# A two-layer hybrid trunk: fewer buffers for split expert weights, more for loaded ones, and attention values with V as the stationary operand

## The chip, the core and the metric

The kernel runs on one core of a Trainium2 chip as one program. The metric is device microseconds of that core, from the start of an execution to its end. Five engines work beside each other: TensorE (PE, with its weight loads shown apart as PEld), VectorE (DVE), ScalarE (ACT), GpSimd (POOL) and SyncE (SP, which issues most DMA transfers).

## The reference, cut to what matters

256 latent and 256 context tokens of width 1024 pass through two layers. Each layer mixes tokens with three groups of heads, and then applies a SwiGLU: a dense one in layer 0, the two best of eight experts in layer 1. The part of the mixer that the change touches, and the expert part:

```python
def gqa_attention(q, k, v):            # 8 query heads, 2 key/value heads, head width 64
    scale = GQA_HEAD_DIM ** -0.5
    def block(qb):
        s = jnp.einsum('bqgrd,bkgd->bgrqk', qb, k) * scale
        p = jax.nn.softmax(s.astype(jnp.float32), axis=-1).astype(v.dtype)
        return jnp.einsum('bgrqk,bkgd->bqgrd', p, v)
    return sweep_query_blocks(block, q)

def moe_swiglu(t, router, wg, wu, wd):
    ...
    for e in range(N_EXPERTS):
        out = out + gates[:, e:e + 1] * swiglu(t, wg[e], wu[e], wd[e])
```

Latent queries read all 512 keys, context queries only the 256 context keys. Layer 1 has latent queries only.

## The kernel before, in words

**Accuracy.** Operands of the large products are split into a high and a low part of type fp32r, and a product is three matmuls (`mm3`, L242 to L245). Softmax weights and values are plain fp32; a plain fp32 matmul is two records (two weight loads and two matmuls) in the trace.

**Grouped-query attention (GQA).** A unit is one query tile (128 queries), one head: 16 units with 512 keys and 16 with 256 in layer 0, 16 with 512 in layer 1. A unit goes through stages of a software pipeline (`staged`, lags 0, 2, 4, 5): `g_scores` computes scores with two matmuls, the first over 128 rows (q high and low against k high, L697), the second over 64 rows (q high against k low, L698), then DVE takes the maximum (L441), ACT the exponential with its sum (L442); `g_turn` transposes the weights, 128 keys at a time, with PE (L458) and copies them to SBUF, by ACT (L434) and DVE (L436) in turn; `g_values` multiplies (L528): the transposed weights are the stationary operand, the 64 columns of V move, one matmul for each 128 keys. The result has queries on partitions. After eight heads `g_finish` divides by the softmax sums (L716, L718), transposes the result four times (L722), and splits it into `yh` and `yl` (L725, L726), which the output projection reads. `take_gkv` prepares K: it splits it and transposes it (L620 to L634); the low part is kept on 64 partitions only (`kgl`, L576).

The Tile scheduler sets the order of this work on each engine from the order in which the program emits it, with Hyena convolution, the norm of the differential heads and, in layer 0, adaLN products (L261) merged in.

**Experts.** 84 rounds and 5 tail rounds run over 672 loads of 512 KB, all issued by SP into a ring of `RAW` buffers (L49, `raw`). A load comes free for the next when its readers are done. Two loads of a round are split, by ACT (`whi`, L1141) and DVE (`wlo`, L1142), into tiles of a ring of three, for experts with a full tile of 128 tokens; the rest of the work (`mm_few`, L1256 to L1263) reads the raw weights, as the moving operand, against 64 or 32 tokens that are stationary in column parts of the array. In `drive` (L1174 to L1216) the order of PE is written out by hand: in a round PE does the split products of the round before (L243 to L245), then the raw products of this round (L1262), while ACT and DVE split for the next. The first load waits for the router's result (SP L1118 reads `ctli`).

Of the kernel before, what the change touches and what calls it, by code (L numbers as in the profile page):

```python
# [10 lines left out]
F32 = mybir.dt.float32  # L11
F32R = mybir.dt.float32r
I32 = mybir.dt.int32
AF = mybir.ActivationFunctionType
# [14 lines left out]
GH, GKV, GD = 8, 2, 64  # L29
# [16 lines left out]
WIDE = {"B": 128, "A": 64, "C": 32}  # L46


RAW = 14  # L49

UPS = [(0, 1024), (1024, 1024), (2048, 1024), (3072, 512)]

# [2 lines left out]
def trunk(ctx: ExitStack, tc: tile.TileContext, I, out, dbg=None):  # L55
# [25 lines left out]
    def merge(*streams):  # L81

        done = [0] * len(streams)
        while True:
            left = [(done[j] / n, j) for j, (_, n) in enumerate(streams) if done[j] < n]
            if not left:
                break
            j = min(left)[1]
            next(streams[j][0], None)
            done[j] += 1  # L90
        for g, _ in streams:
            run(g)
# [5 lines left out]
    def fr(ap):  # L98
        return ap.bitcast(F32)
# [331 lines left out]
    def evac(dst, src):  # L431
        evac_n[0] += 1
        if evac_n[0] % 2:
            S.activation(dst, src, AF.Copy)  # L434
        else:
            V.tensor_copy(dst, src)  # L436
# [28 lines left out]
    def etile():  # L465
        blocks[0] += 1
        if blocks[0] % 9 < 5:
            return wk.tile([128, 512], F32, name="e", tag="e", bufs=5)
        return half_of("aTl").rearrange("p c q -> p (c q)")
# [9 lines left out]
    def keys_of(s):  # L479
        return (0, 4) if s == 0 else (2, 2)  # L480

    def mixer(i, u, streams, pools, begun, first, extra):
# [75 lines left out]
        def d_values(s, qt, h):  # L558
# [4 lines left out]
            if h == DH - 1:  # L563
# [9 lines left out]

        keys = (ap_l if streams == 2 else hp).tile([128, 2, GKV, 512], F32R, name="keys",
                                                   tag="keys" if streams == 2 else "H1")
        kg, kgl = keys[:, 0], keys[0:64, 1]  # L576
        gv = ap_l.tile([128, 4, GKV * GD], F32, name="gv", tag="gv")
        gt_ = [None, None]
        qg = []
# [39 lines left out]

        def take_gkv(t, ps):  # L620
            r = head_norm(ps[:, 0:128].rearrange("p (h d) -> p h d", d=GD), GKV, t, 1)
            st = wk.tile([128, 6, GD], F32R, name="kst", tag="kst", bufs=2)
            s2 = st[:, 0:4].rearrange("p (h a) d -> p h a d", a=2)
            S.activation(s2, r[:, :, None, :].to_broadcast([128, GKV, 2, GD]), AF.Copy)
            V.tensor_sub(st[:, 4:6], r, fr(s2[:, :, 0]))
            ps2 = bank("t", F32R)
            for m in range(2):
                PE.transpose(ps2[:, 128 * m:128 * m + 128], st[:, 2 * m:2 * m + 2].rearrange("p a d -> p (a d)"),
                             identr)
                PE.transpose(ps2[0:64, 256 + 128 * m:384 + 128 * m], st[:, 4 + m], identr)  # L630
            tk = slice(128 * t, 128 * t + 128)
            evac(kg[:, :, tk], fr(ps2[:, 0:256]).rearrange("p (m q) -> p m q", q=128))
            evac(kgl[:, :, tk], fr(ps2[0:64, 256:512]).rearrange("p (m q) -> p m q", q=128))
            evac(gv[:, t], ps[:, 128:256])  # L634

        run(xblock(u, w, OFF_GK, 256, [(t, 0, 256) for t in range(4)], take_gkv))
# [16 lines left out]
        def hy_blocks():  # L653
            for grp in (2, 1, 0):
                pst = [bank("a") for _ in range(2)]
                for k0 in (0, 4):
                    hi, lo = wload(rows_k(w, 256 * grp, 256, k0, k0 + 4), 4, 256)
                    for j in range(2):
                        cs = slice(128 * j, 128 * j + 128)
                        for k in range(4):  # L660
                            mm3(pst[j][:, 0:ntok], (hi[:, k, cs], lo[:, k, cs]),
                                (u[0][:, k0 + k, 0:ntok], u[1][:, k0 + k, 0:ntok]), k0 + k == 0, k0 + k == KC - 1)
                    if k0 == 0:
                        yield
                for j in range(2):
                    ps = pst[j][:, 0:ntok]
                    if grp == 2:
                        short_conv(4 + j, ps, vv[:, j])
                    elif grp == 1:
                        x1 = wk.tile([128, 512], F32, name="x1", tag="t2k", bufs=4)  # L670
                        short_conv(2 + j, ps, x1[:, 0:ntok])
                        V.tensor_mul(vv[:, j], vv[:, j], x1[:, 0:ntok])
                    else:
                        short_conv(j, ps, x0[:, j])
                yield

        ada_tag[0] = "a"
        merge((d_attn, len(d_units) + 3), (hy_blocks(), 6), *extra[0:1])
        qg.append(ap_.tile([128, GH, ntok], F32R, name="qg", tag="X1"))
        for g in range(2):  # L680
            run(xblock(u, w, OFF_GQ + 256 * g, 256, [(t, 0, 256) for t in range(nq)], take_gq(g)))
# [8 lines left out]
        def g_scores(s, qt, h):  # L690
            kt0, nk = keys_of(s)
            n, q0, g = 128 * nk, 256 * s + 128 * qt, h // 4
            keys = slice(128 * kt0, 128 * kt0 + n)
            if h == 0:
                SM[s, qt] = wk.tile([128, GH], F32, name="sm1", tag="sm", bufs=2)
            ps = bank("s")
            PE.matmul(ps[:, 0:n], qg[0][:, h, q0:q0 + 128], kg[:, g, keys], start=True, stop=False)  # L697
            PE.matmul(ps[:, 0:n], qg[0][0:64, h, q0:q0 + 128], kgl[:, g, keys], start=False, stop=True)  # L698
            e = etile()
            softmax_block(ps, n, e, SM[s, qt][:, h:h + 1])  # L700
            E[s, qt, h] = e

        def g_turn(s, qt, h):
            AT[s, qt, h] = to_keys(E.pop((s, qt, h)), keys_of(s)[1])

        def g_values(s, qt, h):
            if h == 0:
                PV[s, qt] = bank("a")
            g = h // 4
            values(PV[s, qt], h, AT.pop((s, qt, h)), gv[:, :, GD * g:GD * g + GD], *keys_of(s))  # L710

        def g_finish(s, qt, h):
            if h < GH - 1:
                return
            sm, ps = SM[s, qt], PV.pop((s, qt))
            V.reciprocal(sm, sm)  # L716
            o = wk.tile([128, 512], F32, name="go", tag="t2k", bufs=4)
            V.tensor_mul(o.rearrange("p (h d) -> p h d", d=GD), ps.rearrange("p (h d) -> p h d", d=GD),  # L718
                         sm[:, :, None].to_broadcast([128, GH, GD]))
            ps = bank("a")  # L720
            for c in range(4):
                PE.transpose(ps[:, 128 * c:128 * c + 128], o[:, 128 * c:128 * c + 128], ident)  # L722
            p3 = ps.rearrange("p (c q) -> p c q", q=128)
            q0 = 256 * s + 128 * qt
            S.activation(yh[:, 4:8, q0:q0 + 128], p3, AF.Copy)  # L725
            V.tensor_sub(yl[:, 4:8, q0:q0 + 128], p3, fr(yh[:, 4:8, q0:q0 + 128]))  # L726
# [409 lines left out]
    newest = [None]  # L1136

    def split_w(raw, a, b):
        hi = mp.tile([128, a, b], F32R, name="whi", tag="whi", bufs=3)
        lo = mp.tile([128, a, b], F32R, name="wlo", tag="wlo", bufs=3)  # L1140
        S.activation(hi, raw, AF.Copy)  # L1141
        newest[0] = V.tensor_sub(lo, raw, fr(hi))  # L1142
        return hi, lo
# [492 lines left out]
```

## Time and profile before

| | us |
|---|---|
| three runs | 1896.03, 1898.89, 1900.34 (median 1898.89) |
| the profiled execution | 1900.39 |
| its span in the trace | 1898.6 |
| PE busy | 1816.5 (96%) |
| DVE busy | 896.3 (47%) |
| ACT busy | 618.9 (33%) |
| GQA of layer 0, with what is merged into it | about 199.8 to 289 |
| GQA of layer 1, with what is merged into it | about 847.4 to 898 |
| loads of the expert part | about 948 to 1871 |

A timeline row gives the start, the length, the engine, the line, the operation, what it writes from what, shapes and a count; what stands in brackets is idle time of that engine ahead of it and what ended it. A row of weight loads (PEld) marks where PE's sequencer has got to, and the distance from one row's start to the next is the pitch. PEclk is the granted clock as a share of full speed.

### The profile page before, as it was taken

How to read it: one execution, taken by the hardware profiler on the slowest of the kernel's cores; microseconds unless marked ns; L12 is line 12 of the kernel's file. 1: busy time of each engine (PE TensorE's matmuls, PEld its weight loads, DVE VectorE, ACT ScalarE, POOL GpSimd, SP SyncE). 2: the span in 40 equal slices, each digit the busy share in tenths (PEclk: the TensorE clock that was granted, in tenths of full speed). 3: DMA queues.
4: the chain of work that ended last, by engine and by line, in shares of the span. 5: the costliest groups of instructions: out<-in, count | busy, mean ns of one | idle time of the engine just before them, and what ended most of it. 6: DMA issues, size and time to landing. Idle time of an engine off the chain costs nothing.

```text
span 1898.6 us, 34294 instructions
## 1 busy us (share of the span) xinstructions
PE 1816.5 (96%) x13638; PEld 1245.6 (66%) x13638; DVE 896.3 (47%) x1507; ACT 618.9 (33%) x1037; POOL 65.0 (3%) x75
## 2 busy tenths in 40 slices
PE   6999999899999998989799999999899999999996
PEld 3778668778888887877666666667555544454442
DVE  3767654765754456686633332323333333233333
ACT  3554433433213334554432222222222222222221
POOL 0200100000000000010000000000000000000002
PEclk9999999999999999999799999999998999999998
DMA  8233323444555553230499999999997999999995
GB/s 317 87 109 112 95 88 130 129 161 144 183 171 167 161 168 111 88 107 18 145 408 407 354 402 373 385 343 364 408 399 268 351 404 404 382 400 409 400 404 200
DMA packets 193631, 481.93 MB, mean 254 GB/s; under 512 B 16911, under 2 KB 59824, under 8 KB 193335
## 3 DMA queue, kind: packets, MB, share of 16 engines
q1 hardware_dynamic: 187929, 471.68, 67.3%
q10 hardware_dynamic: 5246, 6.94, 1.1%
q8 instruction: 109, 1.79, 0.4%
q0 software_dynamic: 288, 1.05, 0.2%
q14 instruction: 59, 0.48, 0.1%
HBM read 474.36 MB, written 5.24 MB: 253 GB/s over the span
## 4 chain that ended last, share of the span: by engine, by line
PE 88%; DVE 4%; DMA 3%; ACT 1%; issue 1%; POOL 1%; SPq 0%; POOLq 0%; DVEq 0%; ACTq 0%
PE ma L1262 24%; PE psa L243 8%; PE psa L245 8%; PE psa L244 8%; PE mb L1262 6%; PE mb L243 4%; PE mb L245 4%; PE mb L244 4%; PE psa L528 3%; PE mq L1440 2%; DMA raw<-in_moe_wd_dram 2%; PE pst L458 2%; PE psa L261 1%; PE mq L1330 1%; PE pss L244 1%
## 5 line engine op out<-in xcount | busy, mean ns | idle before, releaser
L1142 DVE TENSOR_TENSOR wlo<-raw,whi 128x1024 fp32r<-128x1024 f32 x168 | 204.7, 1223 | 300.5 <-ACT whi L1141 283.3
L1262 PE MATMUL ma<-raw,xF 128*32 128x256 f32 (+3 forms) x4352 | 326.2, 385 | 3.7 <-issue 2.9
L1141 ACT ACTIVATE whi<-raw 128x1024 fp32r<-128x1024 f32 x168 | 177.0, 1057 | 379.2 <-PE mb L245 288.3
L1262 PEld LDWEIGHTS ma<-raw,xF 128*32 128x32 f32 (+1 forms) x4352 | 167.2, 115 | 153.5 <-issue 64.1
L235 ACT ACTIVATE whi<-raw 128x1024 fp32r<-128x1024 f32 x120 | 125.3, 1045 | 276.4 <-PE pst L245 84.5
L236 DVE TENSOR_TENSOR wlo<-raw,whi 128x1024 fp32r<-128x1024 f32 x120 | 144.8, 1208 | 118.7 <-ACT whi L235 116.9
L243 PE MATMUL psa<-uh,whi 128*128 128x512 f32 (+1 forms) x448 | 173.1, 388 | 1.8 <-DVE uh L386 1.8
L245 PE MATMUL psa<-uh,wlo 128*128 128x512 f32 (+1 forms) x448 | 171.7, 384 | 2.5 <-DVE wlo L236 2.4
L244 PE MATMUL psa<-ul,whi 128*128 128x512 f32 (+1 forms) x448 | 172.1, 384 | 0.0
L1262 PE MATMUL ma<-raw,hF 128*32 128x256 f32 (+1 forms) x1904 | 165.7, 418 | 6.3 <-DMA raw<-in_moe_wd_dram 5.7
L1262 PEld LDWEIGHTS ma<-raw,hF 128*32 128x32 f32 (+1 forms) x1904 | 73.5, 115 | 89.9 <-issue 32.6
L313 DVE SCALAR_TENSOR_TENSOR acc<-raw,cst,acc 128x512 f32<-128x512 f32 x140 | 98.4, 748 | 28.6 <-DMA raw<-in_w_ada_dram 27.9
L245 PEld LDWEIGHTS psa<-uh,wlo 128*128 128x128 f32 x448 | 84.9, 190 | 20.7 <-DVE wlo L236 5.1
L243 PEld LDWEIGHTS psa<-uh,whi 128*128 128x128 f32 x448 | 85.4, 191 | 19.9 <-DVE uh L386 2.0
L244 PEld LDWEIGHTS psa<-ul,whi 128*128 128x128 f32 x448 | 85.5, 191 | 15.9 <-issue 0.2
L243 PE MATMUL mb<-whi,xB 128*128 128x512 f32 x224 | 95.6, 427 | 0.0
L243 PE MATMUL psa<-whi,uh 128*128 128x256 f32 (+1 forms) x288 | 89.9, 313 | 5.7 <-DVE t L424 3.2
L245 PE MATMUL mb<-whi,xB 128*128 128x512 f32 x224 | 90.5, 404 | 0.0
L244 PE MATMUL mb<-wlo,xB 128*128 128x512 f32 x224 | 90.4, 403 | 0.0
L244 PE MATMUL psa<-wlo,uh 128*128 128x256 f32 (+1 forms) x288 | 88.6, 308 | 1.7 <-DVE wlo L236 1.7
L245 PE MATMUL psa<-whi,ul 128*128 128x256 f32 (+1 forms) x288 | 87.9, 307 | 0.0
L1262 PE MATMUL mb<-raw,xF 128*32 128x256 f32 (+3 forms) x768 | 84.6, 423 | 0.0
(383 smaller groups left out, 2735.9 us busy)
## 6 DMA issues: line engine op xcount, KB each, us to landing
raw<-in_moe_wg_dram SPq DMA_DIRECT2D x224, 512.0 KB, 7.6
raw<-in_moe_wu_dram SPq DMA_DIRECT2D x224, 512.0 KB, 7.6
raw<-in_moe_wd_dram SPq DMA_DIRECT2D x224, 512.0 KB, 9.0
raw<-in_w_ada_dram SPq DMA_DIRECT2D x112, 256.0 KB, 3.8
raw<-in_w_ada_dram SPq DMA_DIRECT2D x40, 512.0 KB, 6.2
raw<-in_w_in_dram SPq DMA_DIRECT2D x36, 512.0 KB, 3.6
raw<-in_ffn_wg_dram SPq DMA_DIRECT2D x22, 512.0 KB, 3.9
raw<-in_ffn_wu_dram SPq DMA_DIRECT2D x22, 512.0 KB, 3.7
```

Of the source, the lines that this page charges most:

```text
L235: S.activation(hi, raw, AF.Copy)
L236: V.tensor_sub(lo, raw, fr(hi))
L243: PE.matmul(ps, l[0], r[0], start=first, stop=False)
L244: PE.matmul(ps, l[0], r[1], start=False, stop=False)
L245: PE.matmul(ps, l[1], r[0], start=False, stop=last)
L313: V.scalar_tensor_tensor(a[:, sl], raw, c, a[:, sl], op0=OP.mult, op1=OP.add)
L458: PE.transpose(ps[:, 128 * c:128 * c + 128], a[:, 128 * c:128 * c + 128], ident)
L528: PE.matmul(ps[:, 64 * h:64 * h + 64], at[:, c], v[:, kt0 + c], start=(c == 0), stop=(c == nk - 1))
L1141: S.activation(hi, raw, AF.Copy)
L1142: newest[0] = V.tensor_sub(lo, raw, fr(hi))
L1262: PE.matmul(o[s * h:s * h + s, n * j:n * j + n], x, w[:, n * h:n * h + n], start=first and j == 0, stop=last, tile_position=(0, s * h), sk ...
L1440: PE.matmul(o, l, m, start=(j == 0), stop=(j == len(ops) - 1))
```

## The change

`RAW` goes from 14 to 16, and the rings of `whi` and `wlo` from three tiles to two. In GQA: the low part of K is kept twice, on all 128 partitions, so the second score matmul has 128 rows; the four transposes of K are of one shape, with one copy instead of two. The weights of four heads (one K/V head) are collected, even heads in one tile and odd heads in another, and only then multiplied: V is now stationary, 64 columns in the left half of the array for even heads and in the right half for odd ones, and 256 columns of weights (two heads of 128 queries) move. The result has head dimensions on partitions, so it isn't transposed; the reciprocals of the sums are instead broadcast by POOL, turned by four fp32 matmuls against the identity, copied, and multiplied in. The diff's core:

```diff
-RAW = 14
+RAW = 16
...
-        kg, kgl = keys[:, 0], keys[0:64, 1]
+        kg, kgl = keys[:, 0], keys[:, 1]
...
-            PE.matmul(ps[:, 0:n], qg[0][0:64, h, q0:q0 + 128], kgl[:, g, keys], start=False, stop=True)
-            e = etile()
+            PE.matmul(ps[:, 0:n], qg[0][:, h, q0:q0 + 128], kgl[:, g, keys], start=False, stop=True)
+            e = wk.tile([128, 512], F32, name="e", tag="e", bufs=5)
...
+            evac(AT[s, qt, h // 4][h % 2][:, 0:nk, h % 4 // 2], ps[:, 0:128 * nk].rearrange("p (c q) -> p c q", q=128))
...
+            for c in range(nk):
+                for p in range(2):
+                    PE.matmul(PV[s, qt][64 * p:64 * p + 64, 256 * g:256 * g + 256], gv[:, kt0 + c, GD * g:GD * g + GD],
+                              at[p][:, c], start=(c == 0), stop=(c == nk - 1), tile_position=(0, 64 * p),
+                              skip_group_check=True)
...
-            o = wk.tile([128, 512], F32, name="go", tag="t2k", bufs=4)
-            V.tensor_mul(o.rearrange("p (h d) -> p h d", d=GD), ps.rearrange("p (h d) -> p h d", d=GD),
-                         sm[:, :, None].to_broadcast([128, GH, GD]))
-            ps = bank("a")
+            rb = wk.tile([128, GH, GD], F32, name="rb", tag="t2k", bufs=4)
+            G.tensor_copy(rb, sm[:, :, None].to_broadcast([128, GH, GD]))
+            pr = bank("a")
             for c in range(4):
-                PE.transpose(ps[:, 128 * c:128 * c + 128], o[:, 128 * c:128 * c + 128], ident)
-            p3 = ps.rearrange("p (c q) -> p c q", q=128)
+                PE.matmul(pr[:, 128 * c:128 * c + 128], rb[:, 2 * c:2 * c + 2].rearrange("p a d -> p (a d)"), ident,
+                          start=True, stop=True)
+            rt = wk.tile([128, 512], F32, name="rt", tag="t2k", bufs=4)
+            evac(rt, pr)
+            V.tensor_mul(rt, rt, ps)
+            p3 = rt.rearrange("p (c q) -> p c q", q=128)
...
-        hi = mp.tile([128, a, b], F32R, name="whi", tag="whi", bufs=3)
-        lo = mp.tile([128, a, b], F32R, name="wlo", tag="wlo", bufs=3)
+        hi = mp.tile([128, a, b], F32R, name="whi", tag="whi", bufs=2)
+        lo = mp.tile([128, a, b], F32R, name="wlo", tag="wlo", bufs=2)
```

**PE in the middle of layer 1's GQA**, before (L697 and L698 are the scores, L458 transposes, L528 values with V moving, L243 and L244 belong to the Hyena convolution, L742 too):

```order
L458 MATMUL pst<-ident,e 128x128 x4
L697 MATMUL pss<-keys,qg 128x512
L698 MATMUL pss<-keys,qg 128x512
L528 MATMUL psa<-gv,two 128x64 x4
L243 MATMUL psa<-vt_7578,c_90 128x256
L243 MATMUL psa<-vt_7578,c_91 128x256
L528 MATMUL psa<-gv,two 128x64
L244 MATMUL psa<-vt_7579,c_90 128x256
L458 MATMUL pst<-ident,two 128x128 x4
```

and after (L709 transposes, L723 values with V stationary, L736 the turned reciprocals; eight L723 belong to four heads):

```order
L723 MATMUL psa<-two,gv 64x256 x3
L709 MATMUL pst<-ident,e 128x128 x4
L697 MATMUL pss<-keys,qg 128x512
L698 MATMUL pss<-keys,qg 128x512
L723 MATMUL psa<-two,gv 64x256 x5
L709 MATMUL pst<-ident,e 128x128 x4
L697 MATMUL pss<-keys,qg 128x512
L698 MATMUL pss<-keys,qg 128x512
L736 MATMUL psa<-ident,rb 128x128 x4
L709 MATMUL pst<-ident,e 128x128 x4
```

Before, values stand in every unit; after, a unit is transposes and scores alone, and values come in pieces once in four units, cut in two here (3 and 5). Over the program there are 160 matmuls L528 of GQA before, and 80 matmuls L723 in 18 pieces after (11 in layer 0, 7 in layer 1).

**PE at the end of layer 1's GQA**, before (L243 to L245 with `whi,yh` open the output projection):

```order
L245 MATMUL psa<-c_91,Y 128x256
L528 MATMUL psa<-gv,two 128x64 x4
L722 MATMUL psa<-ident,go 128x128 x4
L243 MATMUL psa<-whi,yh 128x512
L244 MATMUL psa<-wlo,yh 128x512
```

and after:

```order
L245 MATMUL psa<-c_91,Y 128x256
L723 MATMUL psa<-two,gv 64x256 x8
L736 MATMUL psa<-ident,rb 128x128 x4
L243 MATMUL psa<-whi,yh 128x512
L244 MATMUL psa<-wlo,yh 128x512
```

The last values are twice as many matmuls, and the four matmuls behind them read the sums and not the values.

**ACT in the expert part**, before (L1141 splits, L1398 and L434 copy results of a finished expert block):

```order
L1141 ACTIVATE whi<-raw 128x1024 x2
L1398 ACTIVATE yC<-mb 128x256
L1141 ACTIVATE whi<-raw 128x1024 x2
L1398 ACTIVATE yB<-mb 128x512 x2
L1141 ACTIVATE whi<-raw 128x1024
L434 ACTIVATE ptC<-mq 128x256
```

and after (L1159 splits, L1416 copies):

```order
L1159 ACTIVATE whi<-raw 128x1024 x2
L1416 ACTIVATE yC<-mb 128x256
L1159 ACTIVATE whi<-raw 128x1024
L1416 ACTIVATE yB<-mb 128x512
L1159 ACTIVATE whi<-raw 128x1024
L1416 ACTIVATE yB<-mb 128x512
L434 ACTIVATE ptC<-mq 128x256
```

One split moves behind one copy. On PE and SP the expert part stands in the same order in both.

## Rows read from the trace of the kernel before

**Rows 1.** The page: busy time by engine, and the chain of work that ended last

```profile
PE 1816.5 (96%) x13638; PEld 1245.6 (66%) x13638; DVE 896.3 (47%) x1507; ACT 618.9 (33%) x1037; POOL 65.0 (3%) x75
...
PE 88%; DVE 4%; DMA 3%; ACT 1%; issue 1%; POOL 1%; SPq 0%; POOLq 0%; DVEq 0%; ACTq 0%
```

**Rows 2.** Windows of both layers' GQA; columns as in the first line

```profile
core 0: us, PE busy (x) PEld busy (x) DVE busy (x) ACT busy (x) POOL busy (x), PEclk, DMA share, GB/s
199.80:289.00 89.20, 88.07 (x510) 59.33 (x510) 52.78 (x114) 41.35 (x107) 6.01 (x6) 0.96 0.32 95
847.40:898.00 50.60, 45.43 (x300) 36.37 (x298) 35.84 (x80) 23.97 (x58) 4.04 (x4) 0.93 0.08 25
```

**Rows 3.** PEld timeline in layer 1's GQA: a unit and the start of the next

```profile
871.27 0.97 PEld L528 LDWEIGHTS psa<-gv,two 128*128 128x128 f32 x8 [0.25 <-issue]
872.10 0.48 PEld L458 LDWEIGHTS pst<-ident,two 128*128 128x128 f32 x4
872.54 0.19 PEld L697 LDWEIGHTS pss<-keys,qg 128*128 128x128 f32 x1
872.98 0.18 PEld L698 LDWEIGHTS pss<-keys,qg 64*128 64x128 f32 x1 [0.25 <-issue]
873.41 0.97 PEld L528 LDWEIGHTS psa<-gv,two 128*128 128x128 f32 x8 [0.25 <-ACT Y L769]
```

**Rows 4.** PEld timeline in layer 0's GQA, scores of a unit with 256 keys

```profile
258.40 0.19 PEld L697 LDWEIGHTS pss<-keys,qg 128*128 128x128 f32 x1
258.72 0.18 PEld L698 LDWEIGHTS pss<-keys,qg 64*128 64x128 f32 x1
259.03 0.21 PEld L458 LDWEIGHTS pst<-ident,two 128*128 128x128 f32 x2
```

**Rows 5.** PEld timeline: 128-row fp32r matmuls in sequence, of 256 columns and of 512

```profile
195.03 0.19 PEld L244 LDWEIGHTS psa<-wlo,uh 128*128 128x128 f32 x1
195.15 0.19 PEld L245 LDWEIGHTS psa<-whi,ul 128*128 128x128 f32 x1
...
905.09 0.19 PEld L245 LDWEIGHTS psa<-whi,yl 128*128 128x128 f32 x1
905.32 0.19 PEld L243 LDWEIGHTS psa<-whi,yh 128*128 128x128 f32 x1
```

**Rows 6.** PEld timeline, expert part: fp32 in column halves, 512 columns, then 256

```profile
1565.19 0.14 PEld L1262 LDWEIGHTS ma<-raw,hF 128*64 128x64 f32 x2 [0.29 <-issue]
1565.62 0.14 PEld L1262 LDWEIGHTS ma<-raw,hF 128*64 128x64 f32 x2 [0.29 <-issue]
1566.57 0.19 PEld L243 LDWEIGHTS mb<-whi,xB 128*128 128x128 f32 x1 [0.81 <-issue]
...
1684.85 4.25 PEld L1262 LDWEIGHTS ma<-raw,xF 128*64 128x64 f32 x40
```

**Rows 7.** Timeline at the end of layer 1's GQA, the finish

```profile
896.77 0.68 DVE L718 TENSOR_TENSOR go<-psa,sm 128x512 f32<-128x512 f32 x1
...
897.51 0.42 PEld L722 LDWEIGHTS psa<-ident,go 128*128 128x128 f32 x4 [0.93 <-DVE go L718]
```

**Rows 8.** Groups by shape: POOL's nearest operation of 128x512 in fp32

```profile
L1478 POOL TENSOR_TENSOR fo<-fo,gf 128x512 f32<-128x512 f32 x2 | 2.5, 1268 | 4.0 <-ACT fsq L1477 4.0
```

**Rows 9.** Windows in the expert part (columns as in rows 2)

```profile
1280.00:1290.00 10.00, 10.00 (x142) 6.49 (x146) 3.21 (x4) 2.83 (x5) 0.00 (x0) 1.00 0.80 280
1340.00:1350.00 10.00, 8.11 (x92) 4.00 (x84) 2.79 (x3) 2.48 (x3) 0.00 (x0) 1.00 1.02 407
...
1500.00:1870.00 370.00, 369.85 (x1797) 176.22 (x1794) 118.42 (x133) 92.47 (x118) 1.20 (x3) 1.00 1.02 401
```

**Rows 10.** Timeline in the expert part: a split's two operations

```profile
1568.26 1.06 ACT L1141 ACTIVATE whi<-raw 128x1024 fp32r<-128x1024 f32 x1 [7.54 <-DMA raw<-in_moe_wu_dram]
...
1569.36 2.58 DVE L1142 TENSOR_TENSOR wlo<-raw,whi 128x1024 fp32r<-128x1024 f32 x2 [7.38 <-ACT whi L1141]
```

**Rows 11.** Windows in layer 1's GQA: where the granted clock is low

```profile
850.00:854.00 4.00, 1.50 (x6) 0.95 (x6) 3.41 (x10) 2.48 (x7) 0.90 (x2) 0.73 0.00 0
854.00:858.00 4.00, 4.00 (x15) 2.69 (x16) 2.21 (x5) 1.38 (x3) 1.27 (x2) 0.50 0.00 0
```

More of the change, by code (lines that the diff above doesn't have):

```diff
@@ L621, in take_gkv @@
             r = head_norm(ps[:, 0:128].rearrange("p (h d) -> p h d", d=GD), GKV, t, 1)
[L622 to L625, printed above, removed]
+            st = wk.tile([128, 2, GKV, 2, GD], F32R, name="kst", tag="kst", bufs=2)
+            rr_ = r[:, :, None, :].to_broadcast([128, GKV, 2, GD])
+            S.activation(st[:, 0], rr_, AF.Copy)
+            V.tensor_sub(st[:, 1], rr_, fr(st[:, 0]))
+            sf = st.rearrange("p b h a d -> p (b h) (a d)")
             ps2 = bank("t", F32R)
[L627 to L630, printed above, removed]
+            for m in range(4):
+                PE.transpose(ps2[:, 128 * m:128 * m + 128], sf[:, m], identr)
             tk = slice(128 * t, 128 * t + 128)
-            evac(kg[:, :, tk], fr(ps2[:, 0:256]).rearrange("p (m q) -> p m q", q=128))
-            evac(kgl[:, :, tk], fr(ps2[0:64, 256:512]).rearrange("p (m q) -> p m q", q=128))
+            evac(keys[:, :, :, tk], fr(ps2).rearrange("p (b m q) -> p b m q", m=2, q=128))
             evac(gv[:, t], ps[:, 128:256])
@@ L678, in mixer @@
         merge((d_attn, len(d_units) + 3), (hy_blocks(), 6), *extra[0:1])
+        pair.clear()
+        blocks[0] = 0
         qg.append(ap_.tile([128, GH, ntok], F32R, name="qg", tag="X1"))
@@ L703, in g_turn @@
         def g_turn(s, qt, h):
-            AT[s, qt, h] = to_keys(E.pop((s, qt, h)), keys_of(s)[1])
+            e, nk = E.pop((s, qt, h)), keys_of(s)[1]
+            if h % 4 == 0:
+                AT[s, qt, h // 4] = [wk.tile([128, 4, 2, 128], F32, name="two", tag=tag, bufs=2) for tag in ("aTh", "aTl")]
+            ps = bank("t")
+            for c in range(nk):
+                PE.transpose(ps[:, 128 * c:128 * c + 128], e[:, 128 * c:128 * c + 128], ident)
+            evac(AT[s, qt, h // 4][h % 2][:, 0:nk, h % 4 // 2], ps[:, 0:128 * nk].rearrange("p (c q) -> p c q", q=128))
         def g_values(s, qt, h):
-            if h == 0:
+            if h % 4 < 3:
+                return
+            if h == 3:
                 PV[s, qt] = bank("a")
-            g = h // 4
-            values(PV[s, qt], h, AT.pop((s, qt, h)), gv[:, :, GD * g:GD * g + GD], *keys_of(s))
+            g, at = h // 4, AT.pop((s, qt, h // 4))
+            kt0, nk = keys_of(s)
+            for c in range(nk):
+                for p in range(2):
+                    PE.matmul(PV[s, qt][64 * p:64 * p + 64, 256 * g:256 * g + 256], gv[:, kt0 + c, GD * g:GD * g + GD],
+                              at[p][:, c], start=(c == 0), stop=(c == nk - 1), tile_position=(0, 64 * p),
+                              skip_group_check=True)
         def g_finish(s, qt, h):
```

## The prediction

> **What bounds the kernel now.** I read the page first: PE is busy for 96% of the span, and the chain of work that ended last runs through PE for 88% of it [rows 1]. So a microsecond taken from PE counts unless PE then waits for something else. That is a statement on the whole span, and the change touches three stages, so the windows come next [rows 2]. In layer 0's GQA PE is busy for 88.07 of 89.2 us and DVE for 52.78: there is room under PE. In layer 1's GQA it is 45.43 of 50.6 for PE and 35.84 for DVE: if PE loses 10 us there, the two are equal, and waits between them begin to set the pace. DMA is at 0.32 and 0.08, and bounds neither. The expert part is another matter: PE and the DMA engines are both close to full in most of it, and each has a stretch in which it alone is late [rows 9]: at 1280 to 1290 PE is full and DMA at 0.80, at 1340 to 1350 PE does 8.11 of 10 us and DMA is full. The first expert load waits for the router's result, which lies behind both layers' GQA, so time won in GQA moves the whole expert part forward as it is.
>
> **Scores.** The second score matmul of a unit uses 64 rows of the array. In a unit of layer 1 the weight loads start at 872.54 (L697), 872.98 (L698) and 873.41 (the next): the pair takes 0.87 us, and PE's sequencer stood 0.25 us ahead of L698 and again behind it with no work that it waited for [rows 3]. Where 128-row fp32r matmuls of 512 columns follow each other the pitch is 0.23 [rows 5], so a pair would take 0.46. For 256 keys the pair takes 0.63 (258.40 to 259.03 [rows 4]) against twice 0.12 [rows 5]. After the change both have 128 rows. I take these pitches for the new pair: 32 units save 0.41 us, 13.1, and 16 units save 0.39, 6.2: 19.3 us of PE, 12.8 in layer 0 and 6.6 in layer 1. Bounds: if half of the gap comes from the fp32 neighbours, which stay, 9.7; above, 19.3. I take the upper, since the gap ahead of L698 stands between two matmuls of the same type which differ in rows alone.
>
> The Trainium skill, "TensorEngine Tiling (Array Packing)", Key Properties, says that a change of the tiling mode drains TensorE; the gap ahead of the 64-row matmul agrees with it, and by the rule the upper value is the right one. The same rule speaks against the new values, below.
>
> **Values.** Before, 160 matmuls (L528) are 320 records, eight in a full unit, at a pitch of (872.10 - 871.27) / 8 = 0.104 us [rows 3]: 33.2 us. After, 80 matmuls of 256 columns are 160 records. Before has the same form, fp32 in column halves of the array with 256 columns moving, in the expert part: 40 records in 4.25 us, 0.106 each [rows 6], so 17.0 us. That form is slower by itself at one place: where it ends and a full-array matmul follows, the distance is 0.95 us (1565.62 to 1566.57) instead of the 0.43 from pair to pair (1565.19 to 1565.62) [rows 6], 0.52 lost. The order after has 18 pieces of values, so 18 x 0.52 = 9.4 us. Six of the blocks are cut in two at an odd number, where a matmul has no partner in the other half: its two records then take about 0.42 us instead of 0.21, twelve ends, 2.5 us in all. Sum 28.9, a saving of 4.4 us: 2.8 in layer 0, 1.6 in layer 1. Bounds: with no overlap of the halves every record takes twice as long, 0.21, and the saving turns into a loss of 33.6 + 9.4 - 33.2 = 9.8 us; with free ends of pieces it is 16 us. I stay with 4.4, because the expert part shows this form with these neighbours.
>
> **Finish.** Six times, four transposes become four fp32 matmuls, eight records of 128 columns. Nearest rows: 0.104 for a record of 64 columns [rows 3], so 0.8 us or a little more, against 0.4 for the four transposes: 0.5 x 6 = 3 us more for PE, a third of it in layer 1. DVE has one multiplication as before, and the copy of the turned reciprocals lands on ACT or DVE in turn, 0.6 to 0.7 us. POOL's broadcast has no row; its nearest, 128x512 in fp32, takes 1.27 us [rows 8]. It needs only the sums, which are there when the last exponential is, two or more units ahead of the last values, so it is covered in the middle. At the end of layer 1, where nothing else is left, before shows the multiplication at 896.77 and the transposes at 897.51 [rows 7]; after, the chain behind the last values is multiplication, ACT, DVE, without a turn through PE, but the eight values of 64 columns come later in one piece and at their heels four matmuls. The output projection begins with the first query tile, whose split is long done. I put +1 us there (bounds 0 and +2).
>
> **K's preparation.** Four times a layer: four transposes of one shape, one copy of 512 columns instead of two of 256. Nothing on PE, a few tenths on DVE either way: 0.
>
> **Buffers in the expert part.** Two more raw buffers let two more loads of 512 KB run ahead while PE is the late one (1280 to 1290), and so feed PE two loads longer where DMA is (1340 to 1350) [rows 9]. At 401 GB/s [rows 9] a load takes 1.31 us: at most 2.6 us are won, at least none, if later raw buffers come free later by as much. I take 2. Two split tiles instead of three: a round splits two loads, so the split for a round must now wait until the split products of the round before have read theirs. The split takes 1.06 us on ACT and 2.58 / 2 = 1.29 on DVE [rows 10], for two loads about 3.6 us from the first start to the last end. What covers it is the round's raw products, which PE does in between: in the round around 1560 they end at 1566.57 after about 7 us. So nothing, as long as ACT and DVE are free within some 3 us; without that cover each late microsecond would be paid in 84 rounds. One split also moves behind one ACT copy in the order shown, 0.7 us, covered in the same way.
>
> **The sum.** On PE: 19.3 + 4.4 - 3 = 20.7 us in GQA, 13.6 in layer 0 and 7.2 in layer 1. What is late next: the exponential of a unit needs its maximum from DVE, and PE needs the exponential two units on and a free score bank. A unit of layer 1 shrinks from 2.14 us (871.27 to 873.41 [rows 3]) to about 1.5, and DVE, which had 35.84 us of work in the stage, has that still. So I let a tenth of a microsecond for each of 48 units go back into waits, 5 us, two thirds of it in layer 1. 20.7 - 5 = 15.7; + 2 for the raw buffers, - 1 for the tail of layer 1: 16.7. The profiled execution took 1900.39 (span 1898.6 and 1.8 around it): 1883.7; the median of the runs is 1.5 lower than this execution: 1882.2, say 1882.
>
> **The rivals.**
> *All of PE's gain arrives.* If DVE and ACT never hold PE and pieces of values cost less at their ends: 20.7 + 2.6, and half of the 9.4 at the ends, is 28: 1871. For it: DVE has 36 us of room in layer 0. Against: layer 1.
> *PE waits for DVE and ACT, or its clock falls.* If each of 48 units waits 0.3 us for its maximum or exponential, 14 us go back instead of 5: 1891. In the same direction: at 854 to 858 the granted clock is 0.50, 1.2 of 2.4 GHz, behind a stretch (850 to 854) in which PE was little busy [rows 11]; were a PE with more gaps to stay at that level for 16 us more in the two stages, 8 us are lost. For it: layer 1's ratio [rows 2]. Against: the pipeline is two to five units deep.
> *The halves don't overlap.* Then values cost 9.8 us more than before instead of 4.4 less: 16.7 - 14.2 = 2.5, 1896, no change that can be told: the swap would not do what it says. Against it: 0.106 a record [rows 6].
> The Trainium skill's rule on the mode switch would act here through the pieces' ends; by the row it is 0.52 us a piece, in the sum already. The same page, Performance Considerations, advises the swap with two column tiles for 64 moving columns, and promises twofold speed; no run here shows that yet.
> *Splits hold the split products* (slower). ACT and DVE do other work in a round (copies, the hidden layer), and a split that now starts 3 us later meets it. If PE then waits 0.3 us in each of 84 rounds, 25 us: 1907. It decides from about 3 us of delay in a round, and below that is nothing. For it: the split waits for its DMA in places (7.54 us idle ahead of L1141 [rows 10]). Against: where DMA is late PE waits for it anyway.
>
> **How the numbers follow.** Forecast 0.52 (1877 to 1887); all of the gain 0.18 (1867 to 1877); waits or the clock 0.18 (1887 to 1895); no overlap 0.05 (around 1896); splits 0.07 (1903 to 1912). The forecast is 1882. The range leaves out the last two and a tenth of the rest at its ends: 1869 to 1894. About 0.2%, 3.8 us, can be told from no change: faster 0.87, same 0.06, slower 0.07.
>
> **What would show it.** In the timeline of layer 1's GQA: no idle time ahead of the second score matmul, both at 0.23; records of values at 0.106 within a piece and about 0.5 us lost behind it. In the windows: GQA of layer 0 shorter by 10 to 14 us, of layer 1 by 4 to 7; PE's idle time there ended by ACT's exponential or DVE's maximum. In the expert part: no wait of a split product (L243 to L245) for `wlo`, and a stretch between the first and the last load as long as before or 2 us shorter. The forecast is wrong if records of values take 0.2 us, if PE's idle time in GQA is above 15 us, or if the expert part is longer.

## The result and the profile after

The changed kernel takes 1880.11 us (median of four runs, 1876.20 to 1882.41) against 1899.62 of the kernel before on the same chip: a ratio of 0.9891, 95% interval 0.9868 to 0.9915. Two later comparisons, beside other kernels of this study, gave 1880.72, ratio 0.9908 (0.9895 to 0.9921), and 1881.85, ratio 0.9903 (0.9880 to 0.9925). The forecast was 1882.

The page of the kernel after, busy time by engine and the chain that ended last (beside [rows 1]):

```profile
PE 1797.8 (96%) x13502; PEld 1227.0 (65%) x13502; DVE 899.5 (48%) x1506; ACT 624.5 (33%) x1036; POOL 68.6 (4%) x81
...
PE 87%; DVE 5%; issue 3%; DMA 2%; ACT 2%; POOL 1%; ACTq 0%; POOLq 0%; DVEq 0%; SPq 0%
```

PE lost 18.7 us of busy time and the span 19.2: the share is 96% as before, so PE still sets the time. The two GQA stages, from their first score to the first product of the output projection (windows of the kernel after; columns: length, then busy time and instructions of PE, PEld, DVE, ACT and POOL, PEclk, DMA share, GB/s; beside [rows 2]):

```profile
200.54:283.67 83.13, 78.86 (x474) 47.42 (x474) 57.41 (x123) 43.91 (x111) 8.97 (x10) 1.00 0.36 115
836.95:881.77 44.82, 40.22 (x265) 30.74 (x266) 37.66 (x84) 24.98 (x61) 5.41 (x6) 0.92 0.13 41
```

In layer 0 PE now leaves 4.3 us of the stage unused; over the same cut of the kernel before (199.77 to 296.86) it was 1.1. A unit without values in layer 1 (PEld timeline of the kernel after; beside [rows 3]):

```profile
859.43 0.46 PEld L709 LDWEIGHTS pst<-ident,e 128*128 128x128 f32 x4
859.86 0.19 PEld L697 LDWEIGHTS pss<-keys,qg 128*128 128x128 f32 x1
859.97 0.19 PEld L698 LDWEIGHTS pss<-keys,qg 128*128 128x128 f32 x1
860.29 0.51 PEld L709 LDWEIGHTS pst<-ident,e 128*128 128x128 f32 x4
```

No idle time stands ahead of L698 or behind it. The pair takes 0.43 us (859.86 to 860.29) where it took 0.87, and the whole unit 0.86. A block of values, eight matmuls of four heads (PEld timeline of the kernel after, layer 0; beside [rows 6]):

```profile
245.46 1.49 PEld L723 LDWEIGHTS psa<-two,gv 128*64 128x64 f32 x16 [0.36 <-issue]
247.34 0.20 PEld L709 LDWEIGHTS pst<-ident,e 128*128 128x128 f32 x2 [0.39 <-issue]
```

Sixteen records take 1.49 us, 0.093 each on average, and the weight loads have idle time at both ends of the block, 0.36 and 0.39. Inside the block two loads, one for each half, start together (the same timeline, cut into narrow windows):

```profile
245.73 0.14 PEld L723 LDWEIGHTS psa<-two,gv 128*64 128x64 f32 x2
245.94 0.14 PEld L723 LDWEIGHTS psa<-two,gv 128*64 128x64 f32 x2
246.16 0.14 PEld L723 LDWEIGHTS psa<-two,gv 128*64 128x64 f32 x2
```

The next two come 0.216 us later, so the pitch is 0.108 a record; the average is lower because the first four loads come at once. From the block's first load to the next row it is 1.88 us.

To follow the time through all kernels I cut the span at events that each of them has. Stage A runs from layer 0's first score to the first product of the dense block, stage B from the last transposes of Q in layer 1 (L616) to the first product of the output projection, stage C from there to the first expert load, stage D is the rest. The granted clock falls to 0.50, mostly for 3 to 7 us at a time, at places that differ between executions. From layer 0's first score to the first product of the output projection PE is nearly always busy: e1 and e5 stood at 0.50 there for 10.2 us, 3.4 more than the kernel before, and took 1.6 and 1.5 us longer. So from stage A I subtract half of the time spent at 0.50 in that part (in brackets: the stage as it stands in the trace). Nothing is subtracted from there to the dense block: that part takes 56.2 us in seven of the executions and 58.0 in the other seven, all within 0.04, whether 3.4 or 6.8 us of it stand at 0.50. Of B and C only raw times are given; of D too.

| kernel | A | B | C | D | timed against before |
|---|---|---|---|---|---|
| before | 149.9 (153.3) | 43.45 | 44.0 | 956.7 | |
| after | 141.1 (141.1) | 35.0 | 45.1 | 952.6 | 0.9891 |
| after, again (a1) | 141.3 (141.3) | 35.6 | 45.0 | 950.6 | 0.9908 |
| after, again (a2) | 140.5 (143.9) | 34.3 | 44.2 | 949.8 | 0.9903 |
| e1 buffers | 149.8 (154.9) | 43.5 | 44.0 | 950.3 | 0.9989 |
| e5 two split tiles | 149.7 (154.8) | 43.3 | 43.9 | 953.5 | 1.0000 |
| e2 GQA | 141.1 (142.8) | 34.9 | 45.0 | 953.0 | 0.9927 |
| e3 scores | 141.3 (141.3) | 39.4 | 44.0 | 951.3 | 0.9934 |
| e4 values | 146.1 (154.6) | 38.4 | 45.0 | 953.6 | 0.9980 |
| e8 halves apart | 145.1 (146.8) | 38.4 | 44.9 | 953.5 | 0.9952 |
| e9 odd half first | 140.0 (141.7) | 34.8 | 44.4 | 954.0 | 0.9902 |
| e10 sums first | 138.6 (140.3) | 36.4 | 44.2 | 950.2 | 0.9883 |
| e11 both | 136.8 (136.8) | 35.1 | 44.2 | 950.5 | 0.9874 |
| e12 both, again | 136.8 (136.8) | 35.1 | 44.2 | 950.8 | 0.9879 |

Two things are to be read from it before any experiment. A and B fall by 8.8 and 8.5 us and C rises by 1. (The changed kernel's B spreads from 34.3 to 35.6; the executions at these ends stood at 0.50 for 1.9 and 4.9 us of it.) And D varies from 951 to 957 us in single executions of the kernels that have the same expert part (before, e2, e3, e4), so that the 4.2 us between the two profiles in D can't be put down to the buffers; that takes the timed runs.

### The profile page after: what moved, and what is told of

The parts are those of the page before. It is cut to its first block, busy times and chain, and to the rows that moved or that the text cites. A ratio compares the mean times of both kernels' runs of the same rounds, so it can differ in the third digit from the quotient of the medians.

```text
span 1879.4 us, 34068 instructions
## 1 busy us (share of the span) xinstructions
PE 1797.8 (96%) x13502; PEld 1227.0 (65%) x13502; DVE 899.5 (48%) x1506; ACT 624.5 (33%) x1036; POOL 68.6 (4%) x81
## 4 chain that ended last, share of the span: by engine, by line
PE 87%; DVE 5%; issue 3%; DMA 2%; ACT 2%; POOL 1%; ACTq 0%; POOLq 0%; DVEq 0%; SPq 0%
PE ma L1280 25%; PE psa L243 8%; PE psa L245 8%; PE psa L244 8%; PE mb L1280 6%; PE mb L243 5%; PE mb L245 4%; PE mb L244 4%; PE mq L1458 2%; PE mq L1348 1%; PE pss L244 1%; PE pss L243 1%; PE pss L245 1%; PE psa L723 1%; PE psa L261 1%
## 5 line engine op out<-in xcount | busy, mean ns | idle before, releaser
L1159 ACT ACTIVATE whi<-raw 128x1024 fp32r<-128x1024 f32 x168 | 178.1, 1060 | 418.6 <-PE mb L245 394.0
L243 PE MATMUL psa<-uh,whi 128*128 128x512 f32 (+1 forms) x448 | 174.6, 391 | 1.9 <-DVE uh L386 1.9
L245 PE MATMUL psa<-uh,wlo 128*128 128x512 f32 (+1 forms) x448 | 172.4, 386 | 0.8 <-DVE wlo L236 0.7
L244 PE MATMUL psa<-ul,whi 128*128 128x512 f32 (+1 forms) x448 | 172.9, 386 | 0.0
L243 PEld LDWEIGHTS psa<-uh,whi 128*128 128x128 f32 x448 | 86.7, 194 | 20.3 <-DVE uh L386 2.1
L245 PEld LDWEIGHTS psa<-uh,wlo 128*128 128x128 f32 x448 | 86.1, 193 | 18.6 <-DVE wlo L236 2.6
L244 PEld LDWEIGHTS psa<-ul,whi 128*128 128x128 f32 x448 | 86.3, 193 | 15.8 <-issue 0.2
L243 PE MATMUL psa<-whi,uh 128*128 128x256 f32 (+1 forms) x288 | 89.9, 313 | 5.7 <-DVE t L424 3.1
L243 PE MATMUL mb<-whi,xB 128*128 128x512 f32 x224 | 94.7, 423 | 0.0
L244 PE MATMUL psa<-wlo,uh 128*128 128x256 f32 (+1 forms) x288 | 89.1, 310 | 0.8 <-DVE wlo L236 0.8
L245 PE MATMUL mb<-whi,xB 128*128 128x512 f32 x224 | 89.3, 399 | 0.0
L244 PE MATMUL mb<-wlo,xB 128*128 128x512 f32 x224 | 89.0, 397 | 0.0
L245 PE MATMUL psa<-whi,ul 128*128 128x256 f32 (+1 forms) x288 | 88.4, 308 | 0.0
```

The lines of the kernel that those rows point to most:

```text
L243: PE.matmul(ps, l[0], r[0], start=first, stop=False)
L244: PE.matmul(ps, l[0], r[1], start=False, stop=False)
L245: PE.matmul(ps, l[1], r[0], start=False, stop=last)
```

## The experiments

**e1: the buffers alone.**

```diff
-RAW = 14
+RAW = 16
...
-        hi = mp.tile([128, a, b], F32R, name="whi", tag="whi", bufs=3)
+        hi = mp.tile([128, a, b], F32R, name="whi", tag="whi", bufs=2)
```

> Only RAW 16 and two split tiles; grouped-query attention as before. Theory (the expert part gains by the deeper ring, splits stay covered): the expert part, first load to end, 957.2 us before, takes 2 to 4 us less, the rest as before, so 1895 to 1897 beside 1899. Rival (what the expert part gained after the change, 4.2 us, is chance of the clock's dips): nothing, 1899. Rival (two split tiles hold the split products): slower than before.

1895.70 us (twelve runs) against 1897.85, ratio 0.9989 (0.9979 to 0.9999): 2.1 us less. The expert part gains a little from its buffers.

**e5: two split tiles alone**, RAW 14.

> The kernel before with one edit: two split tiles instead of three, RAW still 14. Theory (PE's raw products cover the later split): no change, 1897 to 1899. Rival (splits hold the products of the next round): 0.1 to 0.3 us in each of 84 rounds, 8 to 25 us slower, and what the two raw buffers gave in the run of both was more than it looked.

1899.42 against 1899.90, ratio 1.0000 (0.9991 to 1.0009): nothing. The later split costs nothing, and by that the gain of e1 is the two raw buffers'; sixteen buffers with three split tiles were not run. It isn't that the smaller ring changes nothing. What SP waits for, ahead of its expert loads, in e5, and then in the kernel before (waits; us in total, times, longest):

```profile
SPq L1133 <- DVE wlo L1142: 306.5, 129, 7.8
SPq L1133 <- PE ma L1262: 106.0, 260, 2.5
```

```profile
SPq L1133 <- PE mb L1262: 213.0, 117, 10.0
...
SPq L1133 <- DVE wlo L1142: 65.4, 33, 3.5
```

With two tiles the split is now the last reader of a raw buffer 129 times, and was 33 times. But SP with a full ring isn't what PE waits for: in the list of waits of e5's expert part there is none of a split product (L243 to L245) for `wlo`.

**e2: GQA alone**, with RAW 14 and three split tiles.

> Only grouped-query attention changed; RAW 14 and three split tiles. Theory: layer 0's GQA, 97.1 us from its first score to the first product of the output projection, takes 83 to 87, layer 1's, 50.5, takes 44.5 to 46; the expert part as before; 1883 to 1885 beside 1899. Rival (the expert part's gain hangs on the earlier start of the part, not on its buffers): 1880.

1884.78 against 1897.85, ratio 0.9927 (0.9915 to 0.9939): 13.1 us less. A and B are those of the kernel after to 0.1 us. With e1's 2.1 the parts make 15.2 of the 17 to 19.5 that the whole was measured at; the difference is within the intervals. The stages add up to about 16, more than the timed 13.1. Something that the column for A leaves out goes the other way: between A and B, 22 to 47 us ahead of B, each of the ten executions with the new scores stood at 0.50 for 3 to 7 us, and none of the other four did. By the half that A shows, that is 2 to 3 us; why it comes isn't shown.

**e3: only the scores.**

```diff
-        kg, kgl = keys[:, 0], keys[0:64, 1]
+        kg, kgl = keys[:, 0], keys[:, 1]
...
-            PE.matmul(ps[:, 0:n], qg[0][0:64, h, q0:q0 + 128], kgl[:, g, keys], start=False, stop=True)
+            PE.matmul(ps[:, 0:n], qg[0][:, h, q0:q0 + 128], kgl[:, g, keys], start=False, stop=True)
```

with K's preparation as in the change.

> Only the low part of K on 128 partitions and the second score matmul with 128 rows; values, finish and buffers as before. Theory (the gap of 0.25 us on either side of the 64-row matmul goes, 19.3 us of PE): 13 to 17 us less in both GQA stages together, 1883 to 1886 beside 1899. Rival (half of the gap belongs to the fp32 neighbours): 6 to 8 less, 1891 to 1893.

1886.20 against 1897.85, ratio 0.9934 (0.9921 to 0.9947): 11.7 us less, between the two theories. The sum had 12.8 for layer 0 and 6.6 for layer 1; A fell by 8.6 and B by 4.1. The PEld timeline says why in layer 0. In e3 the score pair stands ahead of an adaLN piece (L261, four column parts of the array) like this:

```profile
219.28 0.19 PEld L695 LDWEIGHTS pss<-keys,qg 128*128 128x128 f32 x1
219.39 0.19 PEld L696 LDWEIGHTS pss<-keys,qg 128*128 128x128 f32 x1
219.94 0.14 PEld L261 LDWEIGHTS psa<-raw,cst 128*32 128x32 f32 x2 [0.37 <-issue]
```

and the same pair in the kernel before:

```profile
220.11 0.19 PEld L697 LDWEIGHTS pss<-keys,qg 128*128 128x128 f32 x1
220.55 0.18 PEld L698 LDWEIGHTS pss<-keys,qg 64*128 64x128 f32 x1 [0.25 <-issue]
220.97 0.14 PEld L261 LDWEIGHTS psa<-raw,cst 128*32 128x32 f32 x2 [0.24 <-issue]
```

From the second score to L261 it was 0.42 us, and is 0.55. The idle time ahead of L698 is gone, the one behind it is not, because the array changes its shape there in any case; it is even longer. In layer 0's order an L261 stands directly behind the second score in 15 of 32 units. There a pair saves 0.86 - 0.66 = 0.2 us and not 0.41. (With 256 keys: 0.31 becomes 0.33, and the pair saves 0.19.) In layer 1, where no such piece is, the unit did shrink as forecast: 1.75 us in e3 against 2.14. There the second score and the values behind it stand like this in e3:

```profile
859.05 0.19 PEld L696 LDWEIGHTS pss<-keys,qg 128*128 128x128 f32 x1
859.29 1.09 PEld L528 LDWEIGHTS psa<-gv,two 128*128 128x128 f32 x8
860.25 0.48 PEld L458 LDWEIGHTS pst<-ident,two 128*128 128x128 f32 x4
```

The plain fp32 load starts 0.24 us behind the score, with no idle time, so the rival's fp32 neighbours keep nothing of the gap. That B fell by 4.1 and not by 6.6 has another ground: three of the layer's 16 pairs stand ahead of B's first row, which leaves 13 x 0.41 = 5.3. One of these runs into a wait for the exponential that was there already and grows, from 1.38 in the kernel before to 1.69 in e3 (PEld timelines of layer 1, before and then e3):

```profile
880.08 0.31 PEld L458 LDWEIGHTS pst<-ident,e 128*128 128x128 f32 x3 [1.38 <-ACT e L442]
```

```profile
867.40 0.31 PEld L458 LDWEIGHTS pst<-ident,e 128*128 128x128 f32 x3 [1.69 <-ACT e L442]
```

The rest, about 1 us, I didn't follow.

**e4: only the values and the finish** (the changed kernel with the scores, K's preparation and the buffers of before).

> Only values with V stationary in column halves and the new finish; the second score matmul with 64 rows and the buffers as before. Theory (17.0 us in records, 9.4 at the ends of pieces, 2.5 at odd cuts, 3 in the finish, against 33.2): 1 to 2 us less, hidden in part: 1897 to 1899 beside 1899. Rival (ends of pieces are free): 10 us less, 1889. Rival (no overlap of the halves): 12 us more, 1911.

1894.49 against 1897.85, ratio 0.9980 (0.9970 to 0.9989): 3.4 us less (2.1 to 5.7). A fell by 3.8, B by 5.0, and C rose by 1.1: 7.7 in the stages, more than was timed. In this execution 23.9 us of A stood at 0.50, against 13.7 before, and the column for A takes that out, which a timed run doesn't; whether it was so in all twelve runs isn't shown. The rival with no overlap is out; the values save more than the sum had.

**e8: the halves apart.** The same matmuls in blocks of the same size, but neighbours lie in one half:

```diff
-            for c in range(nk):
-                for p in range(2):
+            for p in range(2):
+                for c in range(nk):
```

> The changed kernel with one edit: the values of even heads, all key chunks, come first, and then those of odd heads, so that neighbours lie in the same half of the array but for one place in each block. Same count, same form, same ends of pieces. Theory (the pitch of 0.106 us a record comes from two halves at work at once): 0.21 a record in a run, about 15 us more for PE, 8 to 14 us slower than the changed kernel, 1888 to 1894. Rival (the pitch is the record's own, whatever its neighbour): no change, 1880.

The changed kernel ran once more beside it (a1):

> The changed kernel again, so that the next two stand beside it on one chip: 1880 (1876 to 1883), 17 to 19 us below the kernel before.

1890.12, ratio 0.9952 (0.9938 to 0.9967), against 1880.72 of the changed kernel: 9.4 us slower. A and B each lose 3 to 4 us. The block that was shown above, in e8:

```profile
247.73 2.41 PEld L723 LDWEIGHTS psa<-two,gv 128*64 128x64 f32 x16 [0.36 <-issue]
250.52 0.20 PEld L709 LDWEIGHTS pst<-ident,e 128*128 128x128 f32 x2 [0.39 <-issue]
```

Sixteen records in 2.41 us against 1.49, and 2.79 against 1.88 to the next row. Loads of the same half, inside e8's block:

```profile
248.00 0.14 PEld L723 LDWEIGHTS psa<-two,gv 128*64 128x64 f32 x1
248.22 0.14 PEld L723 LDWEIGHTS psa<-two,gv 128*64 128x64 f32 x1
248.43 0.14 PEld L723 LDWEIGHTS psa<-two,gv 128*64 128x64 f32 x1
```

One record every 0.216 us, the 0.21 of the expectation; in the changed kernel two start in that time. So alternating between the halves is what makes the form fast. The block isn't twice as long because the halves overlap once in it: the odd heads' first load starts at 248.65, the even heads' last one at 249.08. From their first loads to the rows behind them, all pieces together take 28.8 us against 22.7. That is 6 of the 9.4 us; A and B together lose 7, and the rest I can't place.

**e9: the odd heads' half first.**

```diff
-                for p in range(2):
+                for p in (1, 0):
```

> The changed kernel with one edit: within a chunk the odd heads' half comes first, so that a block's first matmul already needs the weights that are copied last, and the scheduler has nothing to let through early. Pieces of values: 13 instead of 18, none cut at an odd number. Theory (an end of a piece costs 0.5 us, a lone matmul 0.2): 5 us less for PE, 2 to 4 us faster than the changed kernel. Rival (the early pieces fill gaps in which PE would wait for an exponential): no change, or 1 us slower.

1881.57, ratio 0.9902 (0.9887 to 0.9917), the changed kernel 0.9908: no change that can be told. The pieces are 13 instead of 18 and none is odd; from their first loads to the rows behind them they take 19.3 us instead of 22.7. Of these 3 us stage A shows 1.3 (141.3 in a1, 140.0). In layer 0's GQA PE waits 1.7 us for `e` in e9, against 0.7 in the kernel after. So in part an early piece of values had stood where PE would have waited for an exponential.

**e10: the sums first.** What the finish needs of the sums stands ahead of the last block of values:

```diff
         def g_values(s, qt, h):
...
+            if h == GH - 1:
+                sm = SM[s, qt]
+                V.reciprocal(sm, sm)
+                rb = wk.tile([128, GH, GD], F32, name="rb", tag="t2k", bufs=4)
+                G.tensor_copy(rb, sm[:, :, None].to_broadcast([128, GH, GD]))
+                pr = bank("a")
...
+                RT[s, qt] = wk.tile([128, 512], F32, name="rt", tag="t2k", bufs=4)
+                evac(RT[s, qt], pr)
```

> The changed kernel with one edit: the reciprocals of a query tile's sums, their broadcast, the four matmuls that turn them and their copy stand ahead of the last block of values, and not behind it, since they need nothing of it. Theory (in layer 1 the second query tile's yh comes late, so the first weights of the output projection come free late, and PE waits 1.2 us for the next split of weights): 44.0 us again from the first product of the output projection to the first expert load (45.1 in the changed kernel), and that first product 0.5 to 1 us earlier; 1878 beside 1880. Rival (the wait for the split has another cause): 45 us there, 1880.

1876.65 against 1898.99, ratio 0.9883 (0.9866 to 0.9899). C is back at 44.2 us, as expected. What cost it was this, in the PEld timeline of the kernel after, behind the first product of the output projection at 881.77:

```profile
884.22 0.19 PEld L243 LDWEIGHTS psa<-whi,yh 128*128 128x128 f32 x1 [0.31 <-ACT yh L743]
...
887.48 0.30 PEld L243 LDWEIGHTS psa<-whi,yh 128*128 128x128 f32 x2 [0.20 <-ACT whi L235]
888.74 0.19 PEld L244 LDWEIGHTS psa<-wlo,yh 128*128 128x128 f32 x1 [0.96 <-DVE wlo L236]
```

PE waits 0.31 us for the second query tile's `yh`; its products are done later, so the weights that they read come free later, the next weights are split later, and PE waits 1.16 us for them. The same three rows, with the same numbers to 0.02, stand in the other executions of the changed kernel (a1 and a2), also in a2, whose C is 44.2 for another reason that I didn't follow. In e10 all that is left of it is one wait of 0.32 us for `wlo`:

```profile
886.15 0.19 PEld L244 LDWEIGHTS psa<-wlo,yh 128*128 128x128 f32 x1 [0.32 <-DVE wlo L236]
```

The other half of the expectation fell: the first product doesn't come earlier, B is 0.8 to 1.4 us longer than in the kernel after and a1. B and C together are 80.6 us, where these two have 80.0 and 80.6 (a2 78.5). A is 2 to 3 us shorter. One place of that can be named, PE's waits in layer 0's GQA for the adaLN weights; the kernel after, then e10:

```profile
PE psa L261 <- DMA raw<-in_w_ada_dram: 2.2, 2, 1.8
PE pst L709 <- ACT e L442: 0.7, 2, 0.5
```

```profile
PE psa L261 <- DMA raw<-in_w_ada_dram: 0.3, 1, 0.3
```

The timed gain, 4 us beside a1's 1880.72, is more than the stages show; the two medians are from two chips, and the intervals of their ratios overlap.

**e11: both edits.**

> The same edit and the odd heads' half first. Theory (pieces of values stand where PE would otherwise wait for an exponential, so fewer ends of pieces only turn into waits): as the run before, within 2 us. Rival (with the finish out of the way the ends saved arrive): 3 to 4 us less than the changed kernel, 1876.

1874.79 against 1898.99, ratio 0.9874 (0.9857 to 0.9890), the fastest kernel of the study. The time allows both expectations: it is 1.9 us below e10's, within the theory's 2, and near the rival's 1876. Stage A speaks for the rival: 136.8 us in e11 and in e12, 1.8 below e10 and 4.3 below the kernel after. But it isn't that there are fewer pieces. e11 has 18, as many as the changed kernel, e10 has 22; in e11 as in e9 none is cut at an odd number, and from their first loads to the rows behind them all pieces take 20.0 us in e11, 24.6 in e10. Why e9 alone turned less of it into time is shown only in part: e11 waits for `e` as long as e9 (1.8 and 1.7 us), but for the adaLN weights 0.3 us, where e9 waits 2.0.

**e12: both edits again, beside the changed kernel on one chip (a2).**

> The kernel of both edits again, beside the changed kernel on one chip. Theory (the stages carry it: 4 us in layer 0, 1 in the tail, nothing in the expert part): 4 to 5 us below the changed kernel. Rival (half of the gain seen was the difference of two chips): 2 us below.

> The changed kernel once more, on the chip of the next run: 1880, ratio to the kernel before 0.990.

1876.36 (1874.74 to 1877.32) against the changed kernel's 1881.85 (1879.84 to 1882.50): 5.5 us less; against before 0.9879 (0.9857 to 0.9900). The first theory is the nearer one for the total, by half a microsecond more than its 4 to 5. Of the 5.5 the stages show 3.7 in A, and B, C and D together are 1.7 longer as they stand. Between A and B, in code that is the same in both, e12 takes 504.9 us and a2 507.3, and I can't tell whether that is more than the clock's dips.

## Why the prediction came out right, and where its steps were off

**The bound.** "PE is the bound, a microsecond taken from PE counts" held: PE's busy time and the span fell by nearly the same. The sum for GQA was 20.7 us of PE less 5 for new waits and 1 for the tail, 14.7; e2 measured 13.1 (11.6 to 16.1 by its interval).

**Scores, 19.3 us.** Too large. In layer 1 the unit shrank by 0.40, the 0.41 of the step. In layer 0 the step took each unit's second gap for a part of the 64-row matmul's price, though the order had an adaLN piece in column parts behind 15 of the 32. Such a boundary keeps its gap whatever the shape of the score. 15 x 0.2 less is 3 us. e3's stages show 8.6 + 4.1 = 12.7 and its timed runs 11.7, so some 4 us more of the 19.3 didn't arrive, and of that the runs place only part (e3 above). The lower bound, 9.7, was nearer, and for another reason than the fp32 neighbours that it named. The section of the Trainium skill that I cited for it ("TensorEngine Tiling (Array Packing)", Key Properties: a change of the tiling mode drains TensorE) agrees with these rows better than my use of it: it ties the drain to the change of mode, and I charged it to one instruction.

**Values, 4.4 us.** Too small. The 0.104 for a record of before was read in a piece whose first load stood behind L698's gap; in e3, without the gap, eight records take 0.96 us (859.29 to 860.25 above), 0.12 each. A record after was sized right: 0.108 where the halves alternate, against 0.106 in the sum, and 0.216 alone in its half (e8), against 0.21. The end of a piece was taken too dear. In layer 1 the blocks of after take 10.8 us together (from the row ahead of a block to the row behind it, less the same distance in a unit without values). 64 records at 0.108 are 6.9 of it and six odd ends at 0.216 are 1.3; the 2.6 that are left make 0.37 for each of the seven ends, by my estimate, and not 0.52. (The idle times of the block's row, 0.36 and 0.39, are those of the weight loads, and PE still works in part of them.) Before, sixteen units of 0.89 (1.75 for a unit of e3 less 0.86 for one without values) took 14.2: 3.4 saved, and 1.6 in the sum. That the halves overlap was right, and decisive: in e8, where they do so only at one place in a block, 9.4 us of the gain are lost. The rival without any overlap stood 14.2 below the forecast.

**Layer by layer.** The two errors lie in different layers, and so the sum holds better than its parts: layer 0 was to give 11.9 net of waits and gave 8.8, layer 1 was to give 3.9 and gave 8.5. That the total came within 2 us of the forecast is in so far luck.

**What is late next.** The forecast had 5 us of new waits, two thirds in layer 1, for DVE's maximum or ACT's exponential. Layer 0 has 3.1 us of new idle time on PE, and 2.2 of them wait for adaLN weights by DMA (row above), which the prediction didn't name; the exponential comes second. Layer 1 has hardly any new.

**The tail, +1.** Right in size (C, 44.0 to 45.1), but not by the mechanism given: not the finish itself is on the path but the weights of the output projection that are freed late behind it.

**Buffers, 2 us and nothing.** Both right: 2.1 (0.2 to 4.0) in e1, 0.0 in e5. That the two buffers feed PE where DMA is late fits PE's waits for expert loads: 6.2 us on average in the five executions with 14 buffers (4.4 to 7.6), 4.7 in the nine with 16 (4.3 to 5.3). The rival in which splits hold the split products is out.

**What was to be seen.** No idle time ahead of L698: seen. Values at 0.106 within a piece and 0.5 behind: 0.108, and some 0.4. Layer 0's GQA shorter by 10 to 14 and layer 1's by 4 to 7 in the windows: 14.0 and 5.7 as they stand, but of the 14.0 3.4 are the clock, which stood at 0.50 for 7 us in that stretch of before, and 1.7 are adaLN transposes that moved behind the cut (the 56.2 and 58.0 us from that cut to the dense block). Both windows would have borne out the forecast of each layer, and the cleaner cut does not.

## What to carry to other kernels

The gap at a change of the array's shape belongs to the boundary and not to the odd instruction: count, in the order, how many boundaries really vanish when one instruction takes its neighbours' shape, and count those that a new shape brings. A small operand made stationary in column halves pays when neighbours alternate between the halves (3.4 us in e4; 9.4 lost in e8). That blocks which aren't cut at odd numbers pay too is seen in stage A alone (e9, e11, e12). The work that only needs the row sums can go ahead of the last block. When a part's price is read from one unit, ask what it hides in a gap that is to vanish: the 0.104 was 0.12 without the gap. And an average over a merged row is not a pitch: the merged rows give 0.093 and 0.15 a record, the distances between the loads 0.108 and, in one half alone, 0.216.

## What the runs showed of the hardware that I had not expected

A column half by itself takes 0.216 us for a record of 256 fp32 columns, and two that alternate take 0.108: the halves work fully beside each other, and in e8 they did so without alternation too, where the run of one half ended and that of the other began. A wait at a shape change isn't additive: between a 64-row score and a column-part piece PE stood 0.24 us, between a 128-row score and the same piece 0.37. And the granted clock falls to 0.50 in stretches of 3 to 7 us at places that differ between executions; two with the same work in a stage differ by microseconds through that alone (a2's stage A is 143.9 as it stands and 140.5 without, the kernel after has 141.1), which is the size of the effects that were to be told apart here. Where PE waits for DVE's norm ahead of the dense block, 3.4 us more or less of it cost nothing: 56.2 us either way.
